# The first block's stages put in order by the timeline model instead of the plain one

## The chip, the core and the metric

The kernel runs on one core of one Trainium2 chip. Its engines each work through a list of instructions of their own, in the order in which the list was written when the program was built: TensorE (PE in the profile, its weight loads PEld), VectorE (DVE), ScalarE (ACT), GpSimd (POOL) and SyncE (SP, which here issues the loads from HBM). The metric is device microseconds (us) of one execution; below it is better.

## What is computed

256 latent tokens of 1024 features, 256 context tokens beside them, batch 1, all in float32. There are two blocks. The first has two layers, each a mixer of three head groups that share one input and one output projection, and then a feed-forward part:

```python
for layer in range(2):
    need_ctx = layer < 1
    hl = modulate(rmsnorm(xl), sh1, sc1); hc = modulate(rmsnorm(xc), csh1, csc1)
    pl, pc = hl @ w_in, hc @ w_in
    na = neighbourhood_attention(q, k, v)   # 8 heads of 64, window and all context keys
    rw = bi_rwkv7(u)                        # 4 heads, both directions, S_t = S_{t-1}(diag(w)+z b') + v k'
    cv = conformer_conv(u)                  # 256 channels, 31 taps, layer norm, silu
    xl = xl + g1 * concat(na, rw, cv) @ w_out         # the same for xc in layer 0
    hl = modulate(rmsnorm(xl), sh2, sc2)
    xl = xl + g2 * (swiglu(hl) if layer == 0 else top2_of_8_experts(hl))
```

The shifts, scales and gates (`sh1`, `sc1`, `g1`, ...) are `silu(c) @ mod_w`. The dense SwiGLU of layer 0 has 2816 hidden features and takes 512 tokens; the experts of layer 1 have 3584 and take the latent tokens alone. The second block has two layers more of gated attention, a spatial gate, a short convolution and a feed-forward part, on the 256 latent tokens.

## The kernel before

Every product with a weight is made in three passes: `wload` splits a float32 weight into a high part `wh` (cast on ScalarE, L174) and a low part `wl` (a subtraction on VectorE or GpSimd, L175), and `proj` adds wh·xH, wh·xL and wl·xH in PSUM (L146 is the line of all matmuls, L150 of all transposes by TensorE). A load brings 256 or 512 columns of eight k tiles.

The mixer of a layer (`mixer`) is cut into parts, each a Python generator, and a string of letters, `SEQ[l]`, says in which order their steps are issued: p the recurrence's elementwise preparation (psprep), x the convolution's columns (psprep too), g the products within a chunk of 64 tokens (psgram, their result S), i the inverses of the triangular blocks (31 dependent steps on VectorE with `pd`, `Xi` and `Ad`, L689 and L691; then transposes into TD, L697, and TN, L699; then small products, psinv), n the columns of queries, keys and values (psnap), c the walk from chunk to chunk (pschain, with the copies RH L795 and UV L803), a the attention (psatt, bias added at L852, maxima `nm` at L854), t the taps of the convolution (`ca`, L891, 30 steps of two instructions on VectorE), m the modulation vectors that come later (psmod), h the norm of each head (pshn), v the convolution's norm (pscv). Then follows the output projection (pswout). The rest of the block is the SwiGLU (psffn; the second layer's first modulation vectors go beside it), the routing (psrout) and the experts (psmoe).

The order of the letters isn't the order on the engines. The kernel is written for a framework that collects the instructions of a block and lists them anew, engine by engine, from their dependencies and from costs that a model gives them; a plain model or, on request, a model of the engines' timelines. A program falls into such blocks where control flow or an explicit block begins: the main block runs from the start to the end of the second expert, where a conditional on the largest expert's size stands (L1291, its body isn't run here); the second holds experts 2 to 7; the last is the second block of the network, opened on its own at L1248 with `with tc.block(schedule_with_timeline_sim=True):`. Before the change, this last one alone asks for the timeline model.

Of the kernel before, what the change touches and what calls it, by code (L numbers as in the profile page):

```python
# [47 lines left out]
# ---- the order in which a mixer's parts are issued, one letter a step: p the recurrence's preparation, g its products  # L48
# within a chunk, i inverses, c from chunk to chunk, h its norm and gates; x the convolution's columns, t its taps, v its
# norm; n the attention's columns (N: low parts on VectorE), a attention; m modulation vectors ----  # L50
# [38 lines left out]
def pack(I):  # L89
    """Lays the inputs out: transposes, reorders and joins, nothing else."""  # L90
# [42 lines left out]
class K:  # L133
# [26 lines left out]
    def ps(self, shape=(128, 512), tag="ax", name=None):  # L160
        """the next of the banks that this use goes round"""
        if self.tags[tag][0] == "=":
            tag = self.tags[tag][1:]
        b = self.tags[tag]
        self.turn[tag] = (self.turn[tag] + 1) % len(b)
        return self.psum.tile(list(shape), F32, tag="b" + b[self.turn[tag]], name=name or self.nm("ps" + self.lab))

    def banks(self, **tags):
        """the eight banks of PSUM by their use"""
        self.tags, self.turn = tags, {t: -1 for t in tags}  # L170

    def split(self, H, L, src, eng=None):
        """src (float32) = H + L with both parts exact for one pass of the tensor engine."""
        self.nc.scalar.copy(H, src)  # L174
        (eng or self.nc.vector).tensor_sub(L, src, H.bitcast(F32))  # L175

    def wload(self, src, nk, nf):
        """One chunk of weights, split: [(H, L)] of at most 1024 columns of all k tiles together."""
# [24 lines left out]
    def bc(self, dst, r):  # L203
        """dst[p, j*128 + t] = r[t, j]: per-token numbers spread over all partitions."""
# [4 lines left out]
    def rsqrt_small(self, pool, src_ps, n, scale, eps):  # L209
        """(scale * src + eps) ** -0.5 for n columns."""  # L210
# [16 lines left out]
    def norm_bc(self, pool, acc, T):  # L227
        """acc [128, T]: sums of squares over the feature tiles -> PSUM [128, T] of 1/rms."""
# [9 lines left out]
    def mod_norm(self, pool, x, toks, b, G, S, H, L, ks=range(KT)):  # L238
        """H + L = x * b * G + S, features on the partitions; toks: [(slice, column of G and S)]."""
# [11 lines left out]
    def proj(self, ps, wH, wL, xH, xL, ks, fs, first, last, tok=slice(None)):  # L251
        """ps += w^T x over the k tiles of this chunk: weights stationary, three exact passes."""
# [6 lines left out]
    def projT(self, ps, wH, wL, xH, xL, ks, toks, first, last):  # L259
        """ps[tok, f] += x^T w: activations stationary."""  # L260
# [7 lines left out]
    def mod(self, l, banks, raw, tmp, tag="mod"):  # L268
        """mod[l][:, f, v]: features on the partitions, f = 48 tiles, v = 0 latent, 1 context. A generator: one load a step."""
        nc, A = self.nc, self.A  # L270
        for b in banks:
            for h in range(2):
                # 16 feature tiles = (s, h, g, j): this half's are 4h .. 4h + 3 of both vectors
# [27 lines left out]
    def gain(self, l, sc0, name, G=None, k0=0, n=8):  # L301
        """norm gain * (1 + scale)"""
# [10 lines left out]
    def build(self):  # L313
# [4 lines left out]
        with ExitStack() as st:  # L318
# [20 lines left out]
            # silu of the conditioning vectors, padded to a column tile  # L339
# [16 lines left out]
    def first(self, s1, st):  # L356
# [16 lines left out]
        for l in range(2):  # L373
# [18 lines left out]
            with pool("pw", "right") as pw:  # L392
# [12 lines left out]
                if not need:  # L405
# [6 lines left out]
                    # the shift's part of the logits and of the normed rows  # L412
# [40 lines left out]
    def mixer(self, l, x, b, X, M, need):  # L453
        """b: 1/rms of each token. X: the pools of x, closed here once x is normed. M: keeps the pools of what is returned."""
# [24 lines left out]
        hw = P0.tile([128, 74], F32, name=self.nm("hw"))   # halves: w0, a0, ln_g, ln_b, the taps  # L479
# [23 lines left out]
        def shifted(ps, j, out, T):  # L503
            """token shift within each sequence, straight from PSUM"""
# [5 lines left out]
        def sigm(dst, src, **kw):  # L510
            """sigmoid by tanh; the caller halves what it adds"""
# [3 lines left out]
        # the recurrence's columns, the first of them begun while half of the norm is still out  # L515
# [67 lines left out]
        def prep():  # L583
# [56 lines left out]
        def conv():  # L640
# [9 lines left out]
        def gram():  # L650
# [20 lines left out]
        def inverse():  # L671
# [1 line left out]
            with pool("PI", "right") as PI:  # L673
# [7 lines left out]
                for t in range(1, 32):  # L681
                    # the rows are independent: two parts, one's product beside the other's sum; rows from 16 on begin at 16
# [38 lines left out]
        def near():  # L721
# [33 lines left out]
        def chain():  # L755
# [1 line left out]
            with pool("PC", "right", bufs=2) as PC:  # L757
                def ready(c):
                    """values and keys of a chunk, their tokens on the partitions"""
# [75 lines left out]
        def attend():  # L835
# [1 line left out]
            for q0, keys in [(TQ - 256, [0, 1, 2, 3])] + ([(0, [0, 1])] if need else []):  # L837
                n = len(keys)
                for qt in range(2):
# [32 lines left out]
                    # the sums of the softmax come in last  # L872
# [9 lines left out]
        def taps():  # L882
            """convolution: 31 taps"""
# [10 lines left out]
        def heads():  # L894
            nonlocal PN
            PN = PNS.enter_context(pool("PN", "right"))
# [39 lines left out]
        def conv_norm():  # L936
# [51 lines left out]
    def bch(self, dst, r, pool):  # L988
        """dst[p, j*128 + t] = r[t, j, p // 64]: per-token, per-head numbers spread over the head's partitions."""
# [7 lines left out]
    def cols(self, w, c0, nf):  # L997
        """columns c0.. of a [1024, .] weight, split"""
# [6 lines left out]
    def fm(self, ch, nf, xH, xL, T, tok=slice(None), ks=range(8)):  # L1005
        """[PSUM [128 features, T tokens]] of each 128 columns, chunk by chunk; ks: the order of the k tiles"""
# [16 lines left out]
    def residual(self, ps, x, f, gate, then):  # L1023
        """x[:, f] += gate * ps"""
# [47 lines left out]
    def moe(self):  # L1072
        tc, nc, A = self.tc, self.nc, self.A
        x = self.x
        with ExitStack() as st:
# [10 lines left out]
            with tc.tile_pool(name="pr", bufs=1) as pr:  # L1086
# [4 lines left out]
                # 1/rms of each token  # L1091
# [11 lines left out]
                # rank of each expert's logit; equal logits go by index  # L1103
# [10 lines left out]
                # slot of each token in its expert  # L1114
# [9 lines left out]
                # tokens on the partitions  # L1124
# [22 lines left out]
            with tc.tile_pool(name="pg", bufs=2) as pg:  # L1147
                # the first loads take the places of what comes later too
# [36 lines left out]
                for e in range(E):  # L1185
# [26 lines left out]
                    if e == 0:  # L1212
# [3 lines left out]
                        # gates: softmax over the two chosen  # L1216
# [39 lines left out]
    def back(self, e, yH, yL, ohT):  # L1256
        """the expert's rows back on their tokens, two feature tiles a time"""
# [8 lines left out]
    def one_hot(self, oh, pos, e, s0):  # L1266
        """oh[t, e, s]: token t holds slot s0 + s of expert e; two experts at once"""
# [4 lines left out]
    def slots(self, oh, ohT, gs, wt, e):  # L1272
        """ohT: the transpose of oh; gs[s, e]: the slot's gate; two experts at once"""
# [14 lines left out]
    def overflow(self, out, hmH, hmL, oh, ohT, gs, pos, wt, over, pg):  # L1288
        """an expert with more than 128 tokens: its slots 128 .. 255, at the tensor engine's own float32"""
# [53 lines left out]
    def scaled(self, x, H, L, g, k):  # L1343
        """H + L = x * g: the norm's 1/rms of each token comes in after the product"""
# [5 lines left out]
    def ahead(self, pe):  # L1350
        """the loads that the second block begins with, and the norm that ends the first block"""
# [294 lines left out]
```

## Time and profile before

| | |
|---|---|
| three runs | 2881.65, 2889.35, 2890.28 us; median 2889.35 |
| span of the profiled execution | 2892.1 us (the page gives no other time of it; it is 2.75 us over the median) |
| PE, DVE, ACT, POOL busy | 95%, 69%, 51%, 12% of the span |
| mean granted clock of TensorE | 0.961 |
| moved by DMA | 585.77 MB |

The stages, by the first and last of their matmuls: norm and the recurrence's columns to 96.9 us; preparation, products within a chunk and inverses to 260.4; the walk over the chunks to 353.2; the rest of attention, norms of the heads and of the convolution to 441.4; output projection to 492.9; SwiGLU to 888.5; the second layer's mixer to 1232; routing to 1245.9; experts to 2292; the second block to the end. In a window's row, a sum of busy time under the window's length is time in which the engine did nothing; the busy time of PE is made from modelled ends, so small gaps are hidden in it.

### The profile page before, as it was taken

Reading aid. Unit: us, or ns where it says so; the run is one execution under the profiler, and the core shown is the slowest. Engines: PE = TensorE matmul, PEld = TensorE weight load, DVE = VectorE, ACT = ScalarE, POOL = GpSimd, SP = SyncE. Lnnn points to the kernel's source line nnn. Section 1 sums busy time; section 2 is a strip of 40 time slices with the busy share of each in tenths; the row PEclk is TensorE's granted clock in tenths of the full one; section 3 lists DMA queues with packets and bytes.
Section 4 is the critical chain, followed back from the end, with each engine's and each line's share of the span. In section 5 each row is a group of like instructions: output and inputs, shape, how many; then the busy total and the mean of one; then the engine's idle time right before and its main releaser. Section 6 shows DMA issues by size and latency. Waiting matters only on the chain. (4 is left out here: it accounts for less than half of the span.)

```text
span 2892.1 us, 42860 instructions
## 1 busy us (share of the span) xinstructions
PE 2758.9 (95%) x17006; PEld 2262.8 (78%) x17006; DVE 1988.5 (69%) x2753; ACT 1468.4 (51%) x2032; POOL 348.4 (12%) x256
## 2 busy tenths in 40 slices
PE   6998999999998879999989999999999999999999
PEld 4677656778886766677867777778777889998999
DVE  4685464323235796488888888888889868856784
ACT  3323243323224332477767776777767646644563
POOL 1420022211001610100000000000000221301120
PEclk9898799999999998899999999999999999999999
DMA  6122155333333234589888999999999835563553
GB/s 226 51 74 74 52 153 190 101 118 95 99 96 105 81 96 133 160 288 356 320 318 321 325 358 333 334 335 362 335 334 341 306 121 175 177 189 117 161 182 111
DMA packets 352321, 585.77 MB, mean 203 GB/s; under 512 B 12656, under 2 KB 180592, under 8 KB 352112
## 3 DMA queue, kind: packets, MB, share of 16 engines
q1 hardware_dynamic: 352112, 582.95, 59.2%
q8 instruction: 136, 2.23, 0.3%
q14 instruction: 73, 0.60, 0.1%
HBM read 580.80 MB, written 2.10 MB: 202 GB/s over the span
## 5 line engine op out<-in xcount | busy, mean ns | idle before, releaser
L175 DVE TENSOR_TENSOR wl<-wr,wh 128x1024 fp32r<-128x1024 f32 x978 | 1169.1, 1224 | 477.9 <-ACT wh L174 464.6
L174 ACT CAST wh<-wr 128x1024 fp32r<-128x1024 f32 x992 | 1003.9, 1044 | 682.0 <-PE psffn L146 193.2
L146 PE MATMUL psmoe<-wh,xH 128*128 128x512 f32 x896 | 355.2, 397 | 3.4 <-ACT wh L174 3.4
L146 PE MATMUL psmoe<-wl,xH 128*128 128x512 f32 x896 | 356.3, 398 | 1.0 <-DVE wl L175 0.5
L146 PE MATMUL psmoe<-wh,xL 128*128 128x512 f32 x896 | 355.2, 396 | 0.0
L146 PEld LDWEIGHTS psmoe<-wl,xH 128*128 128x128 f32 x896 | 168.3, 188 | 45.7 <-DVE wl L175 6.5
L146 PEld LDWEIGHTS psmoe<-wh,xH 128*128 128x128 f32 x896 | 168.7, 189 | 44.2 <-ACT wh L174 5.0
L146 PEld LDWEIGHTS psmoe<-wh,xL 128*128 128x128 f32 x896 | 168.6, 188 | 39.4
L146 PE MATMUL pssf<-oh,wl 128*128 128x256 f32 x704 | 199.2, 283 | 0.0
L146 PE MATMUL pssf<-ohT,wh 128*128 128x256 f32 x704 | 198.9, 283 | 0.0
L146 PE MATMUL pssf<-oh,wh 128*128 128x256 f32 x704 | 198.5, 283 | 0.0
L146 PE MATMUL psmoe<-wh,aL 128*128 128x512 f32 x448 | 178.1, 398 | 2.0 <-DVE aL L175 2.0
L146 PE MATMUL psmoe<-wh,aH 128*128 128x512 f32 x448 | 175.5, 397 | 2.5 <-ACT aH L174 2.5
L146 PE MATMUL psmoe<-wl,aH 128*128 128x512 f32 x448 | 163.1, 399 | 0.0
L1546 POOL TENSOR_SCALAR x<-x,fin 128x256 f32<-128x256 f32 x8 | 12.2, 1542 | 1059.5 <-DVE hmL L1347 1059.5
L146 PE MATMUL psffn<-h2L,wh 128*128 128x512 f32 x352 | 138.6, 394 | 1.3 <-POOL h2L L249 1.3
L146 PE MATMUL psffn<-h2H,wh 128*128 128x512 f32 x352 | 138.0, 394 | 1.0 <-ACT h2H L248 1.0
L146 PE MATMUL psffn<-h2H,wl 128*128 128x512 f32 x352 | 137.4, 391 | 0.0
L146 PEld LDWEIGHTS pssf<-oh,wl 128*128 128x128 f32 x704 | 135.1, 192 | 0.0
L146 PEld LDWEIGHTS pssf<-ohT,wh 128*128 128x128 f32 x704 | 135.0, 192 | 0.0
L146 PEld LDWEIGHTS pssf<-oh,wh 128*128 128x128 f32 x704 | 134.9, 192 | 0.0
L146 PEld LDWEIGHTS psmoe<-wh,aL 128*128 128x128 f32 x448 | 84.1, 188 | 24.3 <-DVE aL L175 4.3
(476 smaller groups left out, 5634.7 us busy)
## 6 DMA issues: line engine op xcount, KB each, us to landing
wr<-moe_w_gate SPq DMA_DIRECT2D x112, 1024.0 KB, 6.9
wr<-moe_w_up SPq DMA_DIRECT2D x112, 1024.0 KB, 6.2
wr<-moe_w_down SPq DMA_DIRECT2D x112, 1024.0 KB, 6.3
wm<-mod_w SPq DMA_DIRECT2D x96, 512.0 KB, 4.2
wr<-f_up SPq DMA_DIRECT2D x44, 1024.0 KB, 5.1
wr<-w_in SPq DMA_DIRECT2D x52, 512.0 KB, 3.8
wr<-w_in SPq DMA_DIRECT2D x16, 1024.0 KB, 5.8
wr<-f_down SPq DMA_DIRECT2D x16, 1024.0 KB, 5.5
```

Source lines behind the costliest of these rows:

```text
L146: i = self.nc.tensor.matmul(out, lhsT, rhs, start=start, stop=stop, **kw)
L174: self.nc.scalar.copy(H, src)
L175: (eng or self.nc.vector).tensor_sub(L, src, H.bitcast(F32))
L1546: nc.gpsimd.tensor_scalar(x[:, k], x[:, k], fin[:, k:k + 1], None, op0=ALU.mult)
```

## The change

One argument: the context of the whole program asks for the timeline model too. No instruction of the network is added or taken away; the engines' lists are written in another order. (Comments of the file go too, which the excerpt leaves out.)

```diff
-    with tile.TileContext(nc) as tc:
+    with tile.TileContext(nc, schedule_with_timeline_sim=True) as tc:
         K(tc, nc, A).build()
```

In the main block 5344 of 6847 rows of TensorE's matmuls stand elsewhere, 1023 of 1452 of VectorE's, 603 of 872 of ScalarE's, 75 of 168 of GpSimd's and 155 of 362 of SyncE's. In experts 2 to 7 some 1586 of 3393 of TensorE's move, none by more than 50 places. In the second block 42 of 4659 move, and three of VectorE's. Three places are shown.

First TensorE in layer 0, where the convolution's columns (psprep with wh or wl), the products within a chunk (psgram) and the queries' and keys' columns (psnap) meet. Before, the products within a chunk stand in one row of thirteen groups, and all of psnap behind them:

```order
L146 MATMUL psgram_1108<-ZR_458,BK_462 128x128 x4
L146 MATMUL psgram_1114<-ZR_458,BK_462 128x128 x4
L146 MATMUL psgram_1120<-ZR_458,BK_462 128x128 x4
L146 MATMUL psgram_1126<-ZR_458,BK_462 128x128 x4
L146 MATMUL psnap_1277<-hH_235,wh_1267 128x512
L146 MATMUL psnap_1277<-hL_236,wh_1267 128x512
L146 MATMUL psnap_1277<-hH_235,wl_1268 128x512
```

The same place now; psnap stands between groups of three of psgram:

```order
L146 MATMUL psnap_1342<-hH_235,wh_1331 128x512
L146 MATMUL psgram_1054<-ZR_458,BK_462 128x128 x4
L146 MATMUL psgram_1060<-ZR_458,BK_462 128x128 x4
L146 MATMUL psgram_1066<-ZR_458,BK_462 128x128 x4
L146 MATMUL psnap_1342<-hL_236,wh_1331 128x512
L146 MATMUL psnap_1342<-hH_235,wl_1332 128x512
```

Of the 384 psnap matmuls of layer 0, 108 now stand before the last psgram, and the other 276 behind it and before the first psinv; before, 192 stood between psgram and psinv and 192 beside or behind psinv. In the second layer 266 stand between psgram and psinv, 245 before.

Next VectorE in layer 0, from the end of the inverses to the first chunk. Before, six low parts of weights and one tap (`ca`) stand between the last transpose and the first copies RH:

```order
L699 STREAM_TRANSPOSE TN_1521<-Xi_1136 32x32x32
L697 STREAM_TRANSPOSE TD_906<-Xi_1136 32x32x32
L175 TENSOR_TENSOR wl_1673<-wr_1670,wh_1672 128x1024
L175 TENSOR_TENSOR wl_1679<-wr_1676,wh_1678 128x1024
L175 TENSOR_TENSOR wl_1789<-wr_1786,wh_1788 128x1024
L175 TENSOR_TENSOR wl_1795<-wr_1792,wh_1794 128x1024
L175 TENSOR_TENSOR wl_3755<-wr_3752,wh_3754 128x1024
L175 TENSOR_TENSOR wl_3761<-wr_3758,wh_3760 128x1024
L891 SCALAR_TENSOR_TENSOR ca_2001<-hpad_216,hw_210,ca_2001 128x512
L795 COPY RH_1931<-pschain_1926 128x128
L795 COPY RH_1938<-pschain_1933 128x128
```

Now five of those low parts stand among the steps of the inverse (two did before, of other weights), and taps, bias sums and maxima of the attention stand before RH:

```order
L891 SCALAR_TENSOR_TENSOR ca_2001<-hpad_216,hw_210,ca_2001 128x512 x15
L852 TENSOR_TENSOR psatt_2507<-psatt_2507,bias_2009 128x256
L891 SCALAR_TENSOR_TENSOR ca_2001<-hpad_216,hw_210,ca_2001 128x512 x2
L854 TENSOR_REDUCE nm_2510<-psatt_2507 128x1
L852 TENSOR_TENSOR psatt_2534<-psatt_2534,bias_2009 128x256
L891 SCALAR_TENSOR_TENSOR ca_2001<-hpad_216,hw_210,ca_2001 128x512 x2
L854 TENSOR_REDUCE nm_2537<-psatt_2534 128x1
L891 SCALAR_TENSOR_TENSOR ca_2001<-hpad_216,hw_210,ca_2001 128x512 x2
L795 COPY RH_1931<-pschain_1926 128x128
L795 COPY RH_1938<-pschain_1933 128x128
```

Counted from the last transpose to RH there are now 24 taps, four bias sums, four maxima and one low part. In the second layer 31 taps stand before the first RH, two before.

Last TensorE at the end of layer 0's mixer, where the norm of the heads (pshn) and of the convolution (pscv) run out and the output projection (pswout) begins. Before, attention and modulation stand among them:

```order
L150 MATMUL psatt_3647<-cst,dw_3645 128x128 x4
L146 MATMUL psmod_3509<-wm_3522,csil 32x256 x4
L150 MATMUL pshn_3607<-cst,bch_3608 128x128 x2
L146 MATMUL psmod_3509<-wm_3528,csil 32x256 x4
L150 MATMUL pshn_3615<-cst,bch_3616 128x128 x2
L146 MATMUL pshn_3623<-sgd_221,lg_27_204 128x256
L146 MATMUL pscv_3674<-ca_2001,ones 128x512 x2
```

Now they have been used up by then (185 of the 240 rows of psatt stand before the end of the walk over the chunks, 59 before), and the last 35 matmuls of pshn stand in one row:

```order
L150 MATMUL pshn_3588<-cst,bch_3589 128x128 x2
L146 MATMUL pshn_3604<-sgd_221,lg_27_204 128x256
L150 MATMUL pshn_3596<-cst,bch_3597 128x128 x2
L150 MATMUL pshn_3607<-cst,bch_3608 128x128 x2
L146 MATMUL pshn_3623<-sgd_221,lg_27_204 128x256
L150 MATMUL pshn_3615<-cst,bch_3616 128x128 x2
L146 MATMUL pscv_3674<-ca_2001,ones 128x512 x2
L146 MATMUL pswout_3764<-mH_3734,wh_3754 128x512
```

Other moves: at the very start VectorE makes two low parts of weights before the gain `G` of the first norm (L307, L309), one of which stood behind it; at the entry of the SwiGLU, the second layer's modulation products stand in the norm's stretch, which were spread over the SwiGLU; in the second layer's preparation GpSimd's power (`rr`, L214) stands ahead of two copies; 14 of the 39 psrout matmuls stand within the output projection. GpSimd makes two of its low parts in layer 0's preparation between its products `BK` (L627, L628), where it made them ahead of the inverse, with four left beside the inverse in both orders.

## Rows read from the trace of the kernel before

**Rows 1.** The page: engines, and the chain that ended last, by line.

```profile
PE 2758.9 (95%) x17006; PEld 2262.8 (78%) x17006; DVE 1988.5 (69%) x2753; ACT 1468.4 (51%) x2032; POOL 348.4 (12%) x256
...
PE psmoe L146 24%; PE pssf L146 13%; PE pssp L146 4%; PE psssg L146 2%; PE pssat L146 1%; DVE wl L175 1%; PE psmoe L150 1%; PE pssat L150 0%; ACT wh L174 0%; DVE moe_out L1245 0%; ACT y L1238 0%; DVE aL L175 0%; ACT aH L174 0%; ACT hmH L1346 0%; ACT moe_out L1378 0%
```

**Rows 2.** Windows: length, busy PE, PEld, DVE, ACT, POOL (instructions), clock, DMA, GB/s.

```profile
96.90:169.90 73.00, 64.35 (x296) 46.86 (x295) 51.00 (x64) 16.11 (x24) 41.90 (x26) 0.77 0.15 44
169.90:260.40 90.50, 78.83 (x640) 69.38 (x640) 64.14 (x141) 22.98 (x34) 10.73 (x4) 0.89 0.22 65
260.40:353.20 92.80, 91.93 (x1001) 65.66 (x1000) 48.98 (x122) 26.22 (x64) 0.00 (x0) 0.80 0.20 64
353.20:441.40 88.20, 84.97 (x592) 44.84 (x591) 58.91 (x134) 40.22 (x113) 22.45 (x20) 0.98 0.48 144
492.90:888.50 395.60, 382.37 (x1742) 305.04 (x1741) 124.91 (x150) 114.40 (x148) 46.12 (x35) 0.98 0.36 109
938.20:1009.10 70.90, 59.41 (x403) 50.37 (x403) 54.71 (x69) 23.58 (x34) 44.68 (x27) 0.90 0.28 82
1009.10:1070.60 61.50, 46.06 (x519) 41.92 (x519) 57.43 (x134) 15.52 (x25) 12.63 (x5) 0.89 0.17 52
1245.90:2292.00 1046.10, 1019.99 (x4544) 817.35 (x4544) 898.09 (x883) 748.98 (x835) 0.00 (x0) 0.99 0.93 335
2292.00:2892.10 600.10, 592.53 (x4822) 576.59 (x4822) 432.35 (x650) 313.41 (x493) 124.18 (x87) 0.99 0.48 155
```

**Rows 3.** Waits of PE, whole span: total us, times, longest.

```profile
PE psinv L146 <- DVE TN L699: 25.5, 4, 14.3
...
PE psprep L146 <- DVE sqk L632: 7.8, 3, 5.0
...
PE psffn L146 <- DVE accx L225: 4.6, 2, 3.6
```

**Rows 4.** Timeline of PE, layer 0: start, duration, idle before in brackets.

```profile
160.05 9.84 PE L146 MATMUL psgram<-ZR,BK 64*128 64x128 f32 x104
...
226.13 3.62 PE L146 MATMUL psinv<-TN,S 32*32 32x32 f32 x126 [5.83 <-DVE TN L699]
```

**Rows 5.** Windows of 10 us at either level of the clock.

```profile
110.00:120.00 10.00, 10.00 (x18) 4.70 (x18) 7.61 (x8) 4.25 (x7) 8.01 (x7) 0.50 0.00 0
170.00:180.00 10.00, 10.00 (x45) 8.26 (x46) 9.87 (x20) 1.65 (x2) 0.00 (x0) 1.00 0.01 2
```

**Rows 6.** Lines of POOL, 96 to 170 us: busy, mean ns, idle before.

```profile
L627 POOL TENSOR_TENSOR BK<-ka,il 64x512 f32<-64x512 f32 x4 | 11.7, 2935 | 4.1 <-ACT il L620 4.0
...
L175 POOL TENSOR_TENSOR wl<-wr,wh 128x1024 fp32r<-128x1024 f32 x2 | 4.7, 2364 | 6.1 <-ACT wh L174 6.1
```

**Rows 7.** The page: the low parts on DVE.

```profile
L175 DVE TENSOR_TENSOR wl<-wr,wh 128x1024 fp32r<-128x1024 f32 x978 | 1169.1, 1224 | 477.9 <-ACT wh L174 464.6
```

**Rows 8.** Timeline, second layer's inverse, POOL and DVE.

```profile
1031.96 0.56 DVE L689 TENSOR_TENSOR pd<-Ad,Xi 128x304 f32<-128x304 f32 x2
...
1032.53 2.39 POOL L175 TENSOR_TENSOR wl<-wr,wh 128x1024 fp32r<-128x1024 f32 x1 [3.01 <-ACT wh L174]
...
1032.98 2.39 DVE L689 TENSOR_TENSOR pd<-Ad,Xi 128x320 f32<-128x320 f32 x2
```

**Rows 9.** Timeline of DVE, layer 0: inverse's end, first chunk, second heads' norm.

```profile
226.10 2.17 DVE L697 STREAM_TRANSPOSE TD<-Xi 32x1024 f32<-32x1024 f32 x1
...
263.92 0.48 DVE L795 COPY RH<-pschain 128x128 f32<-128x128 f32 x2
...
415.00 0.17 DVE L212 TENSOR_SCALAR rm<-pshn 128x16 f32<-128x16 f32 x1 [1.79 <-PE pshn L146]
...
438.63 0.42 DVE L931 TENSOR_TENSOR yn<-yn,pshn 128x256 f32<-128x256 f32 x1 [2.12 <-POOL yn L928]
```

**Rows 10.** Lines of DVE from 260 to 455 us.

```profile
L891 DVE SCALAR_TENSOR_TENSOR ca<-hpad,hw,ca 128x512 f32<-128x512 f32 x60 | 44.6, 759 | 0.5 <-ACT ca L887 0.5
L854 DVE TENSOR_REDUCE nm<-psatt 128x1 f32<-128x512 f32 x16 | 10.9, 679 | 0.0
```

## The prediction

> **What bounds the kernel.** I read the page first. TensorE (PE) is busy for 2758.9 of 2892.1 us, and the chain that ended last runs through psmoe (24%) and pssf (13%) on PE [rows 1]: the kernel is PE's work, and an order can win only what PE stands idle, 133 us in all, and what it loses at the lower of its two clock levels. The windows by stage say where that is [rows 2]. The experts take 1046.1 us with 1020.0 busy at a clock of 0.99, the second block 600.1 with 592.5 busy: nothing to win that a few places of order would bring. The stages with something to win or lose are the two mixers. In layer 0, preparation and products within a chunk (96.9 to 169.9) have 73.00 − 64.35 = 8.7 us idle at a clock of 0.77; inverse and psnap (169.9 to 260.4) 11.7 us idle at 0.89; the walk over the chunks 0.9 us idle, though at 0.80; the stage after it 3.2 us. In the second layer the two stages before the walk have 11.5 and 15.4 us idle. The waits name the causes: 25.5 us in which psinv waited for TN, the last link of VectorE's (DVE's) inverse, and 7.8 us of psprep for sqk [rows 3].
>
> Two rates are needed. At 2.4 GHz (granted clock 1.00) 45 matmuls of 128x512 take 10 us, 0.222 each; at 1.2 GHz (0.50) 18 take 10 us, 0.556 [rows 5].
>
> **The change, part by part.** It adds and removes no instruction. All prices are against the span of 2892.1 us, and the sum goes onto the median of 2889.35, which is 2.75 us lower.
>
> *Start.* Two low parts on DVE before the first norm's gain, 1.224 us each [rows 7], where nothing covers PE: between 0 and +2.4; I take +2.
>
> *Layer 0, preparation to the inverse.* 108 psnap come in front of the last psgram: 108 x 0.222 = 24.0 us of PE. The idle 8.7 us takes part of it. If nothing else gives, psgram ends 24.0 − 8.7 = 15.3 us later than at 160.05 + 9.84 = 169.9 [rows 4], and the inverse with it. On the other side stands the clock: 0.77 over 73 us means that 2 x 0.23 x 73 = 33.6 us ran at 1.2 GHz, and full clock throughout would give back half, 16.8 us. psgram also needs BK from GpSimd (POOL), which makes two low parts between them now, 2 x 2.36 = 4.7 us [rows 6]. So psgram's end moves by −1.5 to +15.3; I take +6, near to POOL's 4.7, since POOL was busy for 41.9 of the 73 us and isn't slack.
>
> Behind it the inverse is DVE's chain: its last transpose ended at 226.10 + 2.17 = 228.3 [rows 9], 58.4 us after psgram. Three more low parts stand among its steps now, 3 x 1.224 = 3.7 us. It ends at 169.9 + 6 + 58.4 + 3.7 = 238. The second part of psinv began at 226.13 and lasted 3.6 us [rows 4]; the walk can begin some 10 us after the transposes, at about 247, where it began at 260.4. PE has less to do meanwhile: the 108 are gone from there, so it waits for TN longer than before, by up to 24 − 13 = 11 us. Start of the walk −13, paid with work that was done earlier; what is saved on the whole is idle time and clock: 8.7 us of gaps filled, half of the 16.8 of clock, less some 5 to 11 us more of waiting for TN. I take −9; bounds −20 and +6.
>
> A rule bears on POOL's low parts. One of them, 2.39 us long, ran from 1032.53, and the pair of DVE products that began at 1032.98 took 2.39 where the pair before took 0.56 [rows 8]. By the Trainium skill (SBUF — State Buffer, "SBUF: two separate sides") GpSimd and VectorE hold a shared pair of ports as a lock for a whole instruction, so that a VectorE operation with two SBUF inputs stands still; the trace agrees with 1.8 us lost there. By it the two low parts moved into the preparation cost DVE as well as POOL, which would make the +6 some +9; beside the inverse there are four in both orders, which changes nothing.
>
> *Layer 0, first chunks.* DVE now passes 24 taps, 4 maxima, 4 bias sums and a low part before RH: 24 x 44.6/60 = 17.8, 4 x 0.68 = 2.7 [rows 10], the sums no dearer than the maxima, 1.2 for the low part: 24 us. RH comes at 238 + 24 = 262, not at 247; before it came at 263.92 [rows 9]. So of 13 us won at the walk's start 2 are left on its chain, and PE has to live from attention and modulation for 15 us. By the order 55 or so small matmuls stand there, about 0.27 each, 15 us: just enough, if attention's own maxima, which sit among the same taps, come in time. Thirty more taps (22 us) follow up to the second chunk's UV. PE's queue is strict: a late `nm` holds a transpose, and all the chunk's products behind it. Nothing lost is the lower bound; 15 + 12 us the upper; I take +7.
>
> *Layer 0, the end.* The attention used up early was what lay beside the norms. From `rm` of the second heads' norm to its last product took 438.63 + 0.42 − 415.00 = 24.1 us [rows 9]; PE's own part of it is 35 x 0.27 = 9.5 us. With nothing beside it, up to 14.6 us stand open (all of the 24.1 being true dependence), none if the company alone made it long. One link in it is POOL's, for which DVE sat 2.12 us before the last product alone [rows 9]; I take 9. The convolution's norm behind it adds 3 in the same way (0 to 5). Sum +12, bounds 0 and +19.
>
> *SwiGLU's entry.* The norm held PE for 4.6 us at accx [rows 3], inside 13.2 us idle of the stage [rows 2]. Modulation moved there fills part: −3, bounds −5 and +2 (the loads of it come ahead of those of the weights).
>
> *Second layer's mixer.* The power on POOL comes earlier, 266 psnap instead of 245 cover the inverse: 21 x 0.12 (the narrower shape at the same rate a column) = 2.5 us; I take −4 of 26.9 us idle. 31 taps before RH, of half the length, 31 x 0.37 = 11.5 us: +2, since here too attention stands beside. The end with 20 pshn in a row: +6 by the ratio 20/35 of the 9, and the convolution's norm. Sum +4, bounds −10 and +15.
>
> *Routing, experts, second block.* Of what moves, nothing is on a new chain: DVE is busy 898 of 1046 us, ScalarE 749, PE 1020 [rows 2]. 0; bounds −6 and +6.
>
> Sum: 2 − 9 + 7 + 12 − 3 + 4 + 0 = +13; 2889.35 + 13 = 2902.
>
> **Rivals.**
>
> (1) *Faster: gaps and clock.* The filled preparation keeps the clock up (16.8 us), the gaps close (8.7), and the tails cost a third of what I say (4 and 2): 2 − 20 + 2 + 4 − 4 − 2 = −18: 2871. For it: 10 us at 110 to 120 ran at 0.50 though PE had work without a break, right behind a stretch of small and halting products. Against it: the wait for TN grows, and after it the clock falls again. By the Trainium skill (TensorE: Matmul & The Clock Gate, Part 1) the gate follows how busy the PE has been lately. No row shows yet whether filling these gaps is enough; by that rule alone the preparation would win its 16.8 us.
>
> (2) *No change.* Nine tenths of the time is PE's work in any order; DVE's taps lie on time that attention covers (+2 for +7), tails half as open (+6 and +3), so that 2 − 9 + 2 + 6 − 3 + 1 = −1: 2888.
>
> (3) *Clearly slower: taps in front of the walk.* The place is DVE between TN and the second UV of both layers. If attention's maxima come too late for PE's queue, the 15 and 12 us of layer 0 and some 8 of the second layer stand open; it decides the sign as soon as over half of those 35 us does. With the tails: 2 − 9 + 27 + 12 − 3 + 12 = +41: 2930.
>
> That the change doesn't reach the first block isn't open: the orders differ there.
>
> **Chances.** This measurement tells 0.3%, about 8.7 us, from no change. My forecast, slower by about 13 us: 0.35; rival (1) 0.30; (2) 0.25; (3) 0.10. The forecast's own range, 2893 to 2915, lies for a sixth within the 0.3%, and some of (2) on the slower side: slower 0.42, within 0.3% 0.27, faster 0.31. The range that leaves out two in ten reaches into (1) and halfway to (3): 2867 to 2922.
>
> **What the profile after would show.** Preparation: clock above 0.77 and idle under 8.7 us in the window that ends with psgram; psgram's end near 176. Inverse: psinv waiting for TN longer than 10 us in layer 0, last transpose near 238. Walk: first RH near 262 with PE busy before it; a wait of psatt for `nm` or of pschain for RH of several us speaks for (3). End: 35 pshn with idle between them, waits on `rr`, `bch` and yn of about 9 us, and pswout behind. Experts and second block within 6 us of 1046.1 and 600.1. I'm wrong if psgram ends at or before 170, or if the stretch from the walk's end to pswout is as short as it was.

## The result, and the profile after

The changed kernel is slower: 2917.23 us (median of 4 runs, 2914.07 to 2920.02) against 2889.82 (4 runs of the kernel before beside it), a ratio of 1.0102 with a 95% interval of 1.0077 to 1.0126. On the chip of a later experiment it was 1.0088 (1.0058 to 1.0119). That is 27 us where 13 were forecast: the sign was right and the time lies in the range, but the forecast size was half of the measured one.

The page's line of the engines, of the profiled execution (2914.07 us, span 2912.3), as in [rows 1]:

```profile
PE 2760.7 (95%) x17006; PEld 2282.9 (78%) x17006; DVE 1980.6 (68%) x2753; ACT 1474.4 (51%) x2030; POOL 343.1 (12%) x256
```

PE is busy for as long as before (2758.9 then), so by this account 18 of the 20 us between the two spans are idle time: 151.6 against 133.2. But busy time hides a second item, since a matmul that takes twice as long at 1.2 GHz is busy too: the four matmuls of pscv in layer 0 took 3.78 us at 1.2 GHz in this kernel, and 1.88 at 2.4 in a kernel below (h_fill). The clock, averaged over the span, is 0.950 against 0.961, which is 2 x 0.050 x 2912 = 291 us at the lower level against 226.

The stages of layer 0, the SwiGLU, the second layer up to the walk, the experts and the second block, which answer to [rows 2]; columns as there:

```profile
99.00:182.90 83.90, 80.72 (x392) 61.57 (x391) 61.54 (x68) 22.38 (x32) 45.98 (x28) 0.92 0.22 62
182.90:243.90 61.00, 54.32 (x555) 47.23 (x554) 60.71 (x150) 19.53 (x32) 4.79 (x2) 0.88 0.39 123
243.90:381.80 137.90, 129.36 (x1313) 84.83 (x1310) 76.13 (x177) 42.60 (x116) 1.84 (x3) 0.86 0.26 81
381.80:448.80 67.00, 50.28 (x281) 28.36 (x280) 27.59 (x73) 20.15 (x56) 19.71 (x17) 0.77 0.32 102
501.50:897.60 396.10, 381.66 (x1742) 304.08 (x1740) 122.90 (x153) 114.76 (x148) 46.82 (x35) 0.98 0.36 109
951.20:1021.40 70.20, 61.34 (x379) 53.12 (x376) 52.54 (x63) 19.20 (x29) 37.78 (x24) 0.85 0.25 76
1021.40:1085.60 64.20, 50.68 (x547) 44.38 (x545) 63.93 (x148) 18.20 (x29) 14.96 (x6) 0.84 0.36 114
1268.00:2298.90 1030.90, 1012.60 (x4544) 820.85 (x4544) 892.49 (x874) 754.41 (x831) 0.00 (x0) 0.99 0.94 337
2298.90:2912.30 613.40, 604.96 (x4824) 588.72 (x4822) 432.74 (x650) 314.20 (x494) 123.48 (x87) 0.97 0.47 152
```

The preparation did close its gaps (83.9 − 80.7 = 3.2 us idle instead of 8.7) and raise its clock (0.92 instead of 0.77). The walk begins 17 us earlier and then takes 137.9 us instead of 92.8; in the 67 us behind it, up to the first product of the output projection, PE is idle for 16.7 us at a clock of 0.77. The experts, of which I expected nothing, take 1030.9 us instead of 1046.1, and the second block takes 613.4 instead of 600.1.

PE's waits of the whole span, total, times and longest (answering to [rows 3]):

```profile
PE psinv L146 <- DVE TN L699: 18.1, 4, 8.9
...
PE psrout L146 <- issue: 10.3, 1, 10.3
PE pshn L150 <- DVE bch L992: 10.2, 8, 3.6
```

psinv waits less for TN, not more. New are pshn's 10.2 us for `bch`, the copy that spreads the norms' scale over the columns; psrout's wait in the routing has grown from 4.2 to 10.3 us.

Since one execution of either kernel differs from the next by some 10 us, I profiled both a second time and set the stages side by side, from the first matmul of one stage to that of the next (us; in brackets how many of them ran at 1.2 GHz):

| stage | before, twice | after, twice | mean difference |
|---|---|---|---|
| start to the recurrence's columns | 29.5, 29.3 | 30.0, 30.4 | +0.8 |
| to the last psgram of layer 0 | 140.1 (38), 141.8 (41) | 152.9 (21), 155.2 (24) | +13.1 |
| to the walk | 90.8 (21), 90.6 (21) | 61.0 (15), 61.0 (14) | −29.7 |
| walk | 92.5 (37), 82.0 (10) | 137.8 (40), 145.9 (54) | +54.6 |
| walk's end to output projection | 88.6 (4), 91.2 (10) | 67.0 (31), 67.1 (34) | −22.9 |
| output projection, SwiGLU | 447.0, 447.9 | 448.8, 446.2 | 0.0 |
| second layer to the walk | 182.1, 181.9 | 187.9, 187.0 | +5.5 |
| walk to output projection's end | 161.2, 159.6 | 163.3, 163.2 | +2.9 |
| routing | 14.1, 14.1 | 19.0, 19.0 | +4.9 |
| experts | 1045.2, 1043.1 | 1030.9, 1030.7 | −13.4 |
| second block, first stage | 90.9 (3), 94.2 (10) | 100.6 (24), 100.6 (24) | +8.1 |
| rest of it | 510.1, 510.2 | 512.8, 511.3 | +1.9 |

The differences sum to +26. Layer 0's mixer has +15 of it: 13.1 − 29.7 + 54.6 − 22.9. In its walk and the stage behind it the same work is done in both kernels, but for a few pieces; it takes 209 us on the mean where it took 177.

The times of whole executions show what the clock is worth. On the chip of the second profiles, 25 executions of the kernel before lie between 2867.88 us at a mean granted clock of 0.973 and 2898.40 at 0.961: 69 us more at 1.2 GHz go with 30.5 us more of time, 0.44 each. The six executions of the changed kernel there have 0.947 to 0.953: by the middles of the two ranges some 98 us more at 1.2 GHz than the kernel before. At 0.4 each, that would be 39 us, more than the whole slowdown. Some of that time is at the lower level while PE mostly waits, and costs less; so this is an upper estimate. But the whole times alone don't show that the new order costs anything except by leaving TensorE at the lower level for longer. The stages have to show it.

### The profile page after: what moved, and what is told of

It is laid out like the page before. It is cut to its first block, busy times and chain, and to the rows that moved or that the text cites. A ratio compares the mean times of both kernels' runs of the same rounds, so it can differ in the third digit from the quotient of the medians.

```text
span 2912.3 us, 42912 instructions
## 1 busy us (share of the span) xinstructions
PE 2760.7 (95%) x17006; PEld 2282.9 (78%) x17006; DVE 1980.6 (68%) x2753; ACT 1474.4 (51%) x2030; POOL 343.1 (12%) x256
## 5 line engine op out<-in xcount | busy, mean ns | idle before, releaser
L146 PE MATMUL psmoe<-wl,aH 128*128 128x512 f32 x448 | 146.0, 400 | 0.0
L146 PE MATMUL psffn<-h2L,wh 128*128 128x512 f32 x352 | 137.9, 392 | 0.0
L146 PE MATMUL psffn<-h2H,wl 128*128 128x512 f32 x352 | 130.8, 390 | 0.0
L146 PEld LDWEIGHTS psmoe<-wh,aH 128*128 128x128 f32 x448 | 83.9, 188 | 21.1 <-ACT wh L174 0.6
```

The costliest lines, as they stand in the source:

```text
L146: i = self.nc.tensor.matmul(out, lhsT, rhs, start=start, stop=stop, **kw)
```

## The experiments

All of them but two start from the changed kernel. A hold is an edge of order alone: what the string's step issues on one engine may not be listed before a given instruction of that engine. The excerpts leave out the lines that note these instructions (`walk_pe` and the like). For reference, ratios to the kernel before: the changed kernel 1.0102 and 1.0088.

**Attention and modulation kept for behind the walk (h_tail).**

```diff
+            if g in "am" and walked: hold.enter_context(tc.issue_after(self.walk_pe))
```

where `walked` is true once the string has no c left and `walk_pe` is the walk's last product.

> The changed kernel, with the attention and modulation steps that the string names after the walk's last chunk queued on TensorE behind the walk's last product, in both layers (186 rows of attention then stand behind layer 0's walk, 58 in the changed kernel). Tails theory (the norms of heads and convolution lost their cover, and the clock fell there): the stretch from the last product of the walk to the first of the output projection gets longer in work but loses its idle time (some 20 us in layer 0, 9 in the second layer, under 5 each after), the clock stays up, and the time falls by 15 to 25 us, to 2892 to 2902. Taps theory (VectorE's taps ahead of the first chunks cost it): within 6 us of 2917, as the taps stay where they are. Preparation theory (products within a chunk 13 us late): within 6 us of 2917.

Measured: 2892.69 us (10 runs, 2878.02 to 2903.78), ratio 1.0029 (1.0009 to 1.0048). Two thirds to seven tenths of the slowdown go. Layer 0's walk, and the stage behind it up to the output projection:

```profile
245.00:331.00 86.00, 77.62 (x968) 58.65 (x966) 59.86 (x137) 22.41 (x56) 0.00 (x0) 0.83 0.05 14
331.00:418.70 87.70, 85.10 (x622) 45.06 (x622) 41.16 (x107) 39.70 (x114) 20.26 (x19) 1.00 0.55 169
```

The stage behind the walk has 87.7 − 85.1 = 2.6 us idle instead of 16.7, at a clock of 1.00. Behind the walk now stand 284 matmuls of attention and 238 of modulation, where the changed kernel has 88 and 92. The tails theory's number came out.

**The same in layer 0 alone (h_tail0)**, the condition with `l == 0 and` ahead of it.

> The changed kernel, with attention and modulation held behind the walk in layer 0 alone. Tails theory, both layers open: two thirds of what holding both layers gave (ratio to the kernel before from 1.010 to 1.003), so a ratio of 1.005 to 1.006. If only layer 0 matters: 1.003; if it is the second layer's: 1.010.

Measured: 2909.28 us (10 runs, 2883.89 to 2919.86), ratio 1.0062 (1.0028 to 1.0096). The expected number came out, but the interval reaches from what both layers gave (1.0029) to beyond the changed kernel's 1.0088: that each layer gives about half isn't shown by the time. The same two stretches of layer 0:

```profile
245.60:339.80 94.20, 86.06 (x967) 65.12 (x966) 60.23 (x137) 22.45 (x57) 0.00 (x0) 0.70 0.04 13
339.80:442.50 102.70, 99.04 (x622) 51.18 (x623) 41.06 (x107) 39.89 (x114) 20.26 (x19) 0.85 0.49 152
```

These two kernels have one and the same order until the second layer's walk, and yet the two stretches take 173.7 us in one execution and 196.9 in the other. (The profile of h_tail is of the fastest of its ten executions, that of h_tail0 of one of its slowest, 2919.62 us.) PE's idle time is nearly equal, 11.0 and 11.8 us; what differs is the granted clock, 0.83 and 1.00 against 0.70 and 0.85, which is 29 us at 1.2 GHz against 87. So 58 us at the lower level go with 23 us here, 0.4 us each. A single profile can't show a gain of 10 us in these stages.

It can be shown where the lower level took as long. The changed kernel's second profile has 88 us of it in its walk and the stage behind, and they take 212.9 us; h_tail0 has 87 and takes 196.9. So the hold in layer 0 wins 16 us there at the same clock. PE's idle time in the two stretches is 28.6 us in the one (25.3 in the first profile of the changed kernel) and 11.8 in the other. It isn't all kept: from the output projection to the second layer, h_tail0 and h_tail take 453.6 and 455.9 us where the changed kernel takes 448.8 and 446.2. Why isn't settled; a third kernel with the hold, h_tailp below, takes 445.0 there.

**The taps kept behind RH (h_taps).**

```diff
+            if g == "t" and self.walk_dve: hold.enter_context(tc.issue_after(self.walk_dve))
```

with `walk_dve` the last RH copy issued when the step is.

> The changed kernel, with each tap queued on VectorE behind the copy RH of the chunk that the string names before it. Taps theory: the first RH comes some 12 us earlier than at 257.5, the walk ends earlier by as much, and the time falls by 10 to 20 us, to 2897 to 2907. Tails theory: the walk ends earlier, and the norms behind it stand as bare as before; taps that are left over fall into the tail; within 8 us of 2917.

Measured: 2924.88 us (4 runs), ratio 1.0141 (1.0106 to 1.0176). The first copies RH of the first and second chunk on DVE, then the windows of the walk and of the stage behind it:

```profile
251.89 0.53 DVE L796 COPY RH<-pschain 128x128 f32<-128x128 f32 x2
...
261.78 0.29 DVE L796 COPY RH<-pschain 128x128 f32<-128x128 f32 x1 [2.29 <-PE pschain L146]
```

```profile
245.70:393.00 147.30, 147.30 (x1356) 92.37 (x1354) 58.12 (x148) 44.88 (x122) 2.16 (x3) 0.81 0.28 87
393.00:468.60 75.60, 47.88 (x237) 27.26 (x236) 51.12 (x108) 18.56 (x49) 22.36 (x17) 0.68 0.21 70
```

RH comes 6 us earlier than at 257.54, the second chunk's 16 us earlier than at 277.6, and the walk is no shorter for it (147.3 against 137.8 and 145.9): PE has attention to do in that time in any case, and is busy throughout. The taps that were held fall behind the walk, where that stage grows to 75.6. No cost of the taps ahead of RH shows; the taps theory falls.

**psnap kept behind psgram (h_gram).**

```diff
+            if g == "n" and self.gram_pe: hold.enter_context(tc.issue_after(self.gram_pe))
```

> The changed kernel, with the queries', keys' and values' columns that the string names behind the products within a chunk queued on TensorE behind the last of these, in both layers (no psnap before the last psgram of layer 0, 108 in the changed kernel). Preparation theory: psgram of layer 0 ends near 172 instead of 183, and the time falls by 10 us or more, to under 2907. Tails theory: psgram ends earlier, but the gaps of the preparation open again (3 us idle to 8 or 9, granted clock from 0.92 to 0.8) and psnap comes back behind it; 0 to 10 us slower, 2917 to 2927.

Measured: 2930.59 us (4 runs), ratio 1.0177 (1.0131 to 1.0223). From psgram's end to the walk, and the walk:

```profile
177.20:262.30 85.10, 77.48 (x642) 68.14 (x641) 62.59 (x141) 23.00 (x34) 9.85 (x4) 0.90 0.23 69
262.30:389.80 127.50, 124.76 (x1388) 77.66 (x1388) 85.10 (x193) 47.88 (x128) 2.16 (x3) 1.00 0.43 137
```

psgram ends at 177.6 instead of 183.2 and 185.8 (the changed kernel's two profiles), and the walk begins at 262.3 instead of 243.9 and 246.6. The gaps of the preparation are open again, as the tails theory had said: from 101.0 to 177.2 PE is idle for 16.6 us, at a clock of 0.75. The interleaving that makes psgram late is a gain; the preparation theory falls. Without psnap in front of it psgram ends 5.6 to 8.2 us earlier, so psnap is some half of the 13 us and not all of it.

**All three holds (h_all).**

> The changed kernel with all three holds. If the three are what the change costs, and each part adds, the time comes to the kernel before or below: 2880 to 2895. If something else of the first block's order costs it (start, entry of the SwiGLU, routing, low parts), or the second block's first stage at the lower clock, 2900 to 2915.

Measured: 2924.79 us (4 runs), ratio 1.0145 (1.011 to 1.0181), above both ranges expected. The stage behind the walk:

```profile
353.40:458.00 104.60, 97.28 (x624) 51.13 (x625) 66.98 (x149) 39.91 (x114) 21.28 (x19) 0.87 0.46 142
```

With psnap behind psgram, taps and attention all behind the walk, the last stage has more than it can hide: 104.6 us. The holds don't add.

**Extra matmuls in the bare norms (h_fill).**

```diff
+        for ins in self.hn_pe[-36:]:
+            with tc.issue_after(ins):
+                pd = self.psum.tile([128, 256], F32, tag="b6", name=self.nm("psfill"))
+                self.mm(pd, self.ident, self.gm, True, True)
```

> The changed kernel, with 36 extra matmuls of 128x256 in each layer, of constants into an unused bank, queued one by one behind the last 36 products of the heads' norms; up to there the order is the changed kernel's, instruction by instruction. They do no useful work. Cover theory (what the bare norms cost is that attention's work is no longer there to do while the norms' own chain of VectorE, ScalarE and GpSimd runs): the stretch from walk's end to output projection stays at 62 us or more in layer 0 (67 in both profiles of the changed kernel), whatever the clock does, and the time at 2905 to 2920. Clock theory (most of it is TensorE's clock at 1.2 GHz for 31 to 34 us of that stretch, and 20 in the second layer, for want of work): the clock stays up there, the stretch falls by 10 us or more in layer 0 and 5 or more in the second, and the time by 12 to 20 us, to 2895 to 2903.

Measured: 2930.83 us (4 runs), ratio 1.0178 (1.0144 to 1.0212). The stage behind the walk in layer 0 and in the second layer:

```profile
382.80:448.80 66.00, 61.01 (x351) 36.16 (x352) 27.84 (x73) 20.35 (x56) 19.73 (x17) 0.97 0.31 100
1202.00:1234.10 32.10, 29.41 (x155) 17.07 (x155) 11.81 (x34) 6.54 (x16) 9.66 (x11) 0.95 0.22 66
```

In layer 0 the clock is 0.97 instead of 0.77, and the stage takes 66.0 us instead of 67.0; in the second layer it is 0.95 instead of 0.64, and 32.1 us instead of 28.2. A clock held up by useless work saves nothing there, which is against the clock theory's number. It doesn't show that the stage is as long as its chain and that the clock costs nothing. The added matmuls are busy for 24.7 us of layer 0's 66.0 and stand in front of the norms' own products on PE: a product whose `bch` was ready at 432.02 began at 432.93, 0.91 us late, behind added matmuls and one product of the norms. In the changed kernel the same product began 0.86 us late, at 1.2 GHz and behind the norms' product alone. What the clock gave back the added work can have taken. PE was busy for 20.1 of the 30.7 us at 1.2 GHz in the changed kernel's stage; half of that, 10 us, is the most that the clock can cost there, by this estimate. Of the cover theory's two numbers the stage's came out. The time, 2930.83, lies above both ranges: the orders behind the added matmuls changed as well, and the SwiGLU took 407.7 us instead of 396 with PE no longer idle than before (14.1 and 14.4 us). What costs it there is open.

**GpSimd's low parts behind the last BK, added to h_tail (h_tailp).**

```diff
+            if low and self.bk_pool: hold.enter_context(tc.issue_after(self.bk_pool))
```

> The changed kernel with attention and modulation held behind the walk in both layers (as in the run that came to 1.003 of the kernel before), and the low parts that GpSimd makes of weights held behind its last BK. If those low parts between the BK are a third or more of why psgram ends 13 us late in layer 0 (they took 2.7 and 2.9 us), psgram's end comes from 184 to 178 or 180, the time to 0.998 to 1.001 of the kernel before: this would be level with it or better, and faster than the changed kernel by 1%. If psnap in front of psgram is all of it, psgram's end stays at 184 and the ratio at 1.003.

Measured: 2894.2 us (12 runs), ratio 1.0048 (1.0026 to 1.007). The last psgram on PE in this kernel, and in h_tail:

```profile
178.95 2.60 PE L146 MATMUL psgram<-ZR,BK 64*128 64x128 f32 x24
```

```profile
183.17 1.16 PE L146 MATMUL psgram<-ZR,BK 64*128 64x128 f32 x8
```

It ends at 181.6 instead of 184.3, 2.8 us earlier, between the two numbers expected, and the whole isn't faster than h_tail. So the low parts between the BK are some fifth of the 13 us.

**The experts alone by the timeline model (e_27)**, in the kernel before:

```diff
+                            XB.enter_context(tc.block(schedule_with_timeline_sim=True))
```

opened at the third expert behind the conditional and closed behind the last.

> The kernel before, with the experts 2 to 7 alone put in order by the timeline model. If the changed kernel's 14 us shorter stage of experts (1031 against 1045) comes from their order, this one wins the 10 us of it that lie in experts 2 to 7 and nothing else changes: 0.2 to 0.5% faster than the kernel before, and under 768 us from the conditional to the last product of an expert, where it was 776. If it was the state in which the first part leaves the chip, no change.

Measured: 2881.71 us (12 runs), ratio 0.9984 (0.9956 to 1.0011): not told from no change, and not the 0.2 to 0.5% expected. The conditional's gap, experts 2 to 7, and the second block's first stage:

```profile
1494.40:1501.20 6.80, 0.32 (x4) 0.14 (x2) 1.93 (x4) 0.00 (x0) 0.00 (x0) 0.83 0.58 195
1501.20:2270.40 769.20, 760.65 (x3404) 616.12 (x3404) 667.84 (x658) 559.41 (x625) 0.00 (x0) 0.99 0.94 340
2270.40:2370.10 99.70, 97.02 (x654) 88.58 (x652) 62.43 (x113) 46.78 (x94) 28.95 (x23) 0.88 0.47 151
```

The gap is 6.8 us instead of 9.6, the experts 769.2 instead of 775.6 and 774.4 (just over the 768 expected): 8 to 9 us won of the changed kernel's 13. So most of the experts' gain is their own order's. The last window gives most of it back, 99.7 us at a clock of 0.88 where the kernel before had 90.9 and 94.2.

**Both kernels again (before2, after2).**

> The kernel before once more, for a second profile of it. If the stages of the first profile are the kernel's own, the experts take 1045 us again and the mixers' stages come within 5 us each; what differs by more between two profiles of one kernel, at another granted clock, can't be laid to the order. The experts at 1031 would mean that the changed kernel's gain there was chance.

> The changed kernel once more, on the chip of the other runs here: the same 1% over the kernel before (2905 to 2920 against some 2885). In its profile the experts take 1031 us again, the norms' tail of layer 0 (walk's last product to output projection) some 65 us at a clock under 0.85; the second block's first stage, which ran at 0.88 in the first profile, at 0.97 or more if that was chance.

Measured: 2887.74 (one run) and 2914.83 (6 runs, ratio 1.0088). The walk of layer 0 and experts 2 to 7 of the kernel before:

```profile
261.70:343.60 81.90, 80.85 (x999) 57.94 (x999) 48.93 (x122) 26.14 (x64) 0.00 (x0) 0.94 0.23 72
1507.10:2281.50 774.40, 762.00 (x3404) 609.46 (x3404) 667.18 (x652) 553.89 (x620) 0.00 (x0) 1.00 0.94 339
```

The walk and the stage behind it of the changed kernel:

```profile
246.60:392.40 145.80, 133.56 (x1310) 87.40 (x1310) 76.11 (x177) 42.62 (x115) 1.84 (x3) 0.81 0.24 77
392.40:459.50 67.10, 50.73 (x280) 28.69 (x280) 27.47 (x73) 20.15 (x55) 19.72 (x17) 0.75 0.31 101
```

The walk of one and the same order took 92.5 us at a clock of 0.80 in the first profile and 81.9 at 0.94 in this one. The experts' 13 us repeat to within 2. The second block's first stage stayed at 0.88, against what I expected of after2; over all profiles it ran at 1.2 GHz for 24 us in five of the ten executions whose experts were put in order by the timeline model, and for 3 to 7 in the other five. What decides that isn't settled: the stage's own order is all but the same.

## Why the prediction was right in sign and half in size

By the table's means the parts came to: start +0.8 (forecast +2); preparation and inverse 13.1 − 29.7 = −16.6 (−9); first chunks and end of layer 0, which are the walk and the stage behind it, 54.6 − 22.9 = +31.7 (7 + 12 = 19); output projection and SwiGLU 0.0 (−3); second layer's mixer +8.4 (+4); routing, experts and second block +1.5 (0). So the step that was mis-sized most is what lies from layer 0's first chunk to its output projection: 12.7 us too little, of the 13 that are missing. The other errors nearly cancel.

*Start*, +2: measured +0.8.

*Preparation and inverse*, −9. psgram's end was forecast at 176 and came at 183.2, near the upper bound of 185.2:

```profile
182.05 1.16 PE L146 MATMUL psgram<-ZR,BK 64*128 64x128 f32 x8
...
228.52 0.28 PE L146 MATMUL psinv<-TN,S 32*32 32x32 f32 x4 [1.96 <-DVE TN L699]
...
234.60 3.62 PE L146 MATMUL psinv<-TN,S 32*32 32x32 f32 x124 [2.63 <-DVE TN L699]
```

I took +6 "near to POOL's 4.7", as if the later of two causes counted. Both count: without psnap in front psgram ends 6 to 8 us earlier (h_gram), and the products BK are late as well. The last of them on POOL before:

```profile
145.33 1.72 POOL L628 TENSOR_TENSOR BK<-kd,il 64x512 f32<-64x512 f32 x1
```

and after, the first `aa`, the two low parts and the last product:

```profile
116.11 1.20 POOL L513 TENSOR_SCALAR aa<-aa 128x512 f32<-128x512 f32 x2 [12.08 <-ACT aa L512]
...
123.11 2.73 POOL L175 TENSOR_TENSOR wl<-wr,wh 128x1024 fp32r<-128x1024 f32 x1
...
139.78 2.86 POOL L175 TENSOR_TENSOR wl<-wr,wh 128x1024 fp32r<-128x1024 f32 x1 [0.54 <-ACT wh L174]
...
155.64 1.78 POOL L627 TENSOR_TENSOR BK<-ka,il 64x512 f32<-64x512 f32 x1
```

147.1 against 157.4 at its end: of these 10.4 us 5.6 are the two low parts, longer than the 4.7 forecast, and the rest is older: the first `aa` began at 116.11, 5.0 us later than in the kernel before. Of psgram's own delay the low parts are less, 2.8 us (h_tailp). The walk's start, forecast at 247, came at 243.9, by a second error: I had POOL's low parts beside the inverse at four in both orders; only two of them still ran behind psgram's end, so DVE lost less (wl with pd, [rows 8]; from psgram's end to the last transpose its 61 pd took 18.2 us, 23.6 before), and the last transpose came 53.5 us behind psgram where I had put 62:

```profile
234.58 2.17 DVE L697 STREAM_TRANSPOSE TD<-Xi 32x1024 f32<-32x1024 f32 x1
...
257.54 0.48 DVE L795 COPY RH<-pschain 128x128 f32<-128x128 f32 x2
...
277.60 0.27 DVE L795 COPY RH<-pschain 128x128 f32<-128x128 f32 x1
```

So psinv waited 4.6 us in layer 0 and not "longer than 10". With the walk's start 17 us earlier where 13 were forecast, the two errors are on opposite sides, and the step as a whole came out better than forecast, within its bounds.

*First chunks*, +7: RH was put at 262 and came at 257.54. The price was wrong: h_taps took the taps away from there and the walk got no shorter. The forecast's own arithmetic, 15 us of small matmuls for 15 us of waiting, was right, and its lower bound of nothing the better choice.

*The end of layer 0*, +12: this is the step that carried the forecast's sign. From `rm` to the norms' last product, all of it with nothing beside, on all engines:

```profile
425.12 0.17 DVE L212 TENSOR_SCALAR rm<-pshn 128x16 f32<-128x16 f32 x1 [1.93 <-PE pshn L146]
425.37 2.92 POOL L214 TENSOR_TENSOR rr<-rm,mhalf 128x16 f32<-128x16 f32 x1 [8.22 <-DVE rm L212]
428.32 0.29 DVE L992 COPY bch<-rr 128x256 f32<-128x256 f32 x1 [3.03 <-POOL rr L214]
...
428.67 0.69 PE L150 MATMUL pshn<-cst,bch 128*128 128x128 f32 x2 [3.59 <-DVE bch L992]
...
444.45 0.42 DVE L931 TENSOR_TENSOR yn<-yn,pshn 128x256 f32<-128x256 f32 x1 [0.90 <-POOL yn L928]
```

19.8 us here; POOL's power takes 2.92, DVE waits it out, PE waits 3.6 for what DVE then makes. PE's idle time behind the walk, 16.7 us where it was 3.2, is the forecast's +12 with its mechanism. Keeping attention and modulation for this chain in layer 0 alone gave back 16 us of the two stretches at the same clock (h_tail0), and by the times 8 to 12, which their intervals don't tell from nothing. How much of the bare stage's length is the chain and how much the clock, h_fill doesn't decide. What I didn't see is the other half of the same step: the attention that is missing behind the walk stands in the walk and makes that longer, with 8.5 us of gaps there instead of 0.9 and, on the mean of the two profiles of each kernel, 23 us more at the lower clock, at 0.4 some 9 us. I had put the clock at nothing in both.

*SwiGLU's entry*, −3: 396.1 and 393.7 against 395.9 and 396.8, −1.5. *Second layer's mixer*, +4: measured +8.4. Holding its attention too brought the ratio from 1.0062 to 1.0029, 9 us by the medians, though the two intervals overlap; that the reason is layer 0's is likely and not shown apart.

*Routing, experts, second block*, 0 with bounds of ±6: here the prediction failed, in both directions, and that the sum of +1.5 lies within the bounds is luck. The routing costs +4.9 in every profile of a timeline order. On DVE, from the mean square's row `rm` to the one-hot `oh` that PE waits for, before:

```profile
1235.44 0.16 DVE L212 TENSOR_SCALAR rm<-psrout 128x2 f32<-128x2 f32 x1 [1.82 <-PE psrout L146]
...
1241.84 1.21 DVE L175 TENSOR_TENSOR wl<-wr,wh 128x1024 fp32r<-128x1024 f32 x1
...
1245.09 0.68 DVE L1269 TENSOR_TENSOR oh<-cst,pos 128x512 fp32r<-128x512 f32 x1
```

and after:

```profile
1254.41 0.15 DVE L212 TENSOR_SCALAR rm<-psrout 128x2 f32<-128x2 f32 x1
1254.48 2.35 DVE L175 TENSOR_TENSOR wl<-wr,wh 128x1024 fp32r<-128x1024 f32 x2
...
1258.33 1.21 DVE L175 TENSOR_TENSOR wl<-wr,wh 128x1024 fp32r<-128x1024 f32 x1
...
1267.13 0.69 DVE L1269 TENSOR_TENSOR oh<-cst,pos 128x512 fp32r<-128x512 f32 x1
```

9.7 us became 12.7; 2.4 of the 3 are low parts for the first expert, three instead of one, that stand between. Two more stand right in front of `rm`, and DVE has no gap there. I had seen them in the order and argued that nothing is on a new chain; DVE's place in front of `oh` is one. The experts won 13.4 us, which I had excluded with "a few places of order": it isn't idle time alone that fell, from 26.1 to 18.3 us, but the busy time, from 1020.0 to 1012.6. And the second block gave 10 back, 8 of them in its first stage, which ran at the lower clock for 24 us instead of 3 and 10.

Of the rivals, (1) was right that the preparation's clock comes up with its gaps filled. Of the lower level's 33.6 us there 2 x 0.08 x 83.9 = 13.4 were left, which agrees with the rule cited there from the Trainium skill (TensorE: Matmul & The Clock Gate, Part 1), though the second block's first stage, busy and yet at 1.2 GHz for 24 us, isn't explained by it as told there. It wasn't enough to make the kernel faster: by the table preparation and inverse have 23.5 us fewer at that level on the mean, and walk and bare norms 49 more. (3) gave 2930, no farther from the measured time than the forecast's 2902, but its mechanism isn't there: no cost of the taps shows (h_taps).

One reading of the prediction is off without bearing on the sum: the 0.556 us at 1.2 GHz is the mean of a window of mixed matmuls (most of its time is ten of 64x512 at some 0.83 us each), not the rate of 128x512.

## What to carry to other kernels

Work that can be done at any time is cover: before a scheduler is allowed to bring it forward, ask which chain will be bare at the end, and hold back as much as that chain needs (here 196 matmuls of attention and 146 of modulation in layer 0; with the second layer's 0.6 to 0.7% of the time). The timeline model's order, which fills gaps as they come, gained in the experts and the preparation here and lost at the end of the mixers; one switch for the whole program mixes the two. And profile both kernels twice before laying 10 us to an order, and compare stretches that had the lower clock for as long.

## What I hadn't expected of the hardware

One order, executed twice, differed by 23 us over 190 in the mixer (h_tail and h_tail0) and by 10.5 in the walk of the kernel before, with the granted clock as the difference that the rows show: 2.4 or 1.2 GHz for a part of the stretch, at about 0.4 us lost for each us at the lower level. PE was busy for 97 of 100.6 us of the second block's first stage and still ran 24 of them at 1.2 GHz; in the changed kernel's first profile the clock fell at 2307.7, behind 24 matmuls of 128x2 in 4.1 us and a gap of 0.33 us.
